# Second mixer of a two-layer decoder: the last gate projection ahead of the second group's scan, and each tile's output chain behind its own chunk

## The chip, the cores and the metric

The kernel runs on one core of a Trainium2 chip. The time is the device time of one execution in microseconds; 3108.14 us is the median of three runs. The core has five engines with instruction streams of their own: TensorE (PE: matmuls and transposes), VectorE (DVE), ScalarE (ACT), GpSimd (POOL) and SyncE (SP), which issues most DMAs. An engine works through its stream in order and waits at an instruction until the semaphores that it names have come.

## The reference

Two layers over 512 tokens of width 1024. In layer 0 the token mixer is a sparse attention, in layer 1 a Mamba-2 scan (SSD); each runs beside a cross-attention of four heads into 256 memory tokens, one output projection takes both, and a PEER block (retrieval of single-neuron experts) follows. The change lies in layer 1:

```python
z, xbc, dt_raw, q_mem = jnp.split(h @ b_w_in[j], B_SPLITS, axis=-1)
...
xbc = jax.nn.silu(causal_depthwise_conv(xbc, conv_w, conv_b))
...
y = ssd_scan(xh, dt, a, bm, cm) + xh.astype(jnp.float32) * d[..., None]
y = y.reshape(b, s, SEQ_WIDTH) * jax.nn.silu(z.astype(jnp.float32))
return rms_norm(y, out_norm).astype(z.dtype)
...
mem_out = memory_attention(q_mem, mem_n, w_mem_kv[i])
x = x + jnp.concatenate([seq_out, mem_out], axis=-1) @ w_o[i]
```

The scan has 12 heads in two groups of 6, and is done in four chunks of 128 tokens; a chunk needs the state that the chunk before it left.

## The kernel before

Tokens are four tiles of 128 (t = 0 to 3). A matmul in full precision is three matmuls of a high and a low half (L70, L71, L72). Layer 1 keeps the normed input transposed (`hT`, a high and a low half), and its steps are emitted in the order of a string, `B_ORDER`, which `run_steps` reads. The framework's scheduler takes the emission order as priority and fixes each engine's stream at build; so a step's instructions end up woven into those of other steps.

The steps: `x(j)` projects a block of 128 columns, convolves it, applies SiLU and transposes it (L679, to `xtm`). `decay(t,g)` makes a chunk's decay factors for group g. `z(1)` and `z(2)` project 256 gate columns each for all four tiles, in two halves of two tiles, evicted by ScalarE (L658, to `zs`). `mem(t)` is the cross-attention of a tile, in two halves of two heads: scores (L331, L332), row maximum (L333), exponential (L337, to `P`), transposes (L341), their eviction (L343, to `PT`), weighted sums into the bank `po` (L347), and the division (L351, to `om`). `chunk(t,g)` is a chunk of the scan: the product of the chunk's C and B (L788), times the decay (L789), the diagonal part into `po` (L792), added to `xtm` (L795); from the second chunk on the part of the state (L798, L800, L802); and but for the last chunk the state's update (L807 to L812). `silu()` applies SiLU to the gates of all four tiles (L704). `out(t)` is a tile's output chain: the gates (L817, GpSimd), the sum of squares (L108, ScalarE), the norm's factor (L96 to L104, with a power on GpSimd, L98), its application (L821), six transposes (L363) and the split into `hT` (L83 by ScalarE, L84 by VectorE). `om_T(t)` transposes the attention's output into `hT`. SiLU and Exp are in different tables of ScalarE, so each change from one to the other is a table load.

PSUM has eight banks, which this layer shares out by kind of use; each kind takes its banks in turn, in the order of emission:

```python
self.use_banks(mm=(4, 5, 0), tr=(6, 7), po=(1,), z=(2, 3))
```

`tr` serves the transposes of the softmax (`mem`), of the output chain (`out`) and of `om_T`; a bank is free again when what was read from it has been read. The sum of squares of `out(t)` writes its squares into one of the three `w_raw` buffers, into which the weight blocks of the output projection are loaded too:

```python
self.sumsq(ss, y, self.scratch()[:, :SW])
```

Behind the steps comes `out_proj`, which accumulates all four tiles over eight blocks of `hT`, the two blocks of `om` (6 and 7) first (`acc`).

Of the kernel before, what the change touches and what calls it, by code (L numbers as in the profile page):

```python
# [35 lines left out]
class Trunk:  # L36
# [522 lines left out]
    def attend(self, work, t, j, qS, kS, bias, v, mask, o):  # L559
# [49 lines left out]
        else:  # L609
# [3 lines left out]
        yield  # L613

    B_ORDER = ("qm(0) decay(0,0) x(6) x(1) x(8) qm(1) decay(1,0) x(0) x(2) decay(2,0) x(7) decay(3,0) x(9) chunk(0,0) "
               "x(3) chunk(1,0) chunk(2,0) z(1) chunk(3,0) decay(0,1) decay(1,1) x(4) x(5) decay(2,1) decay(3,1) mem(0) "
               "chunk(0,1) mem(1) chunk(1,1) mem(2) chunk(2,1) mem(3) z(2) chunk(3,1) om_T(0) om_T(1) silu() out(0) "
               "out(1) om_T(2) om_T(3) out(2) out(3)")

    def layer_b(self):  # L620
        self.use_banks(mm=(4, 5, 0), tr=(6, 7), po=(1,), z=(2, 3))
# [656 lines left out]
```

## Time and profile before

| | |
|---|---|
| median of 3 runs | 3108.14 us (3108.0 to 3112.97) |
| the profiled execution | 3111.33 us |
| its span | 3109.6 us |
| PE busy | 2993.3 us, 96% |
| DVE busy | 2319.9 us, 75% |
| ACT busy | 1288.6 us, 41% |
| POOL busy | 963.0 us, 31% |
| mean granted TensorE clock | 0.988 |

The rows below are of this one execution; times in them are microseconds from the span's start. In a timeline a row begins with start and duration; neighbours on one engine overlap a little, so the step from one start to the next is shorter than the duration. What stands in brackets is the idle time before, and what ended it. In PE's rows a full-precision operand of 4 bytes shows as two passes, so a count there can be twice the program's.

### The profile page before, as it was taken

The numbers are of one execution on the slowest core, as the hardware profiler recorded it, in microseconds if no ns is written. First come the engines' busy times: TensorE is split into PE (matmuls) and PEld (weight loads), VectorE is DVE, ScalarE is ACT, GpSimd is POOL, SyncE is SP. The second block draws the span as 40 slices with busy tenths as digits, with TensorE's granted clock in tenths as the row PEclk, the third lists the DMA queues.
The fourth block names the chain that finished last, engine by engine and source line by source line (L and its number), as shares of the span: only waits on it lengthen the run. The fifth ranks groups of instructions, "written<-read, shape, count | busy, mean of one in ns | idle before, by whom it ended". The sixth has DMA issues, their size and how long they took to land.

```text
span 3109.6 us, 44049 instructions
## 1 busy us (share of the span) xinstructions
PE 2993.3 (96%) x16033; PEld 2585.1 (83%) x16038; DVE 2319.9 (75%) x4553; ACT 1288.6 (41%) x2021; POOL 963.0 (31%) x699
## 2 busy tenths in 40 slices
PE   8899999989999999999999999999999999999998
PEld 7788767778999999999978777667799999999997
DVE  5954899857777777777767659995677777777776
ACT  5574327633333333333345632584333333333332
POOL 3312320003333334444313333001233333444440
PEclk9999999999999999999999999999999999999999
DMA  4311226888888889898721122579789988889983
GB/s 162 104 40 55 75 88 247 312 278 294 310 306 306 303 308 322 305 311 305 235 91 62 50 82 69 184 283 324 258 303 311 321 306 307 305 302 314 319 287 104
DMA packets 235154, 718.61 MB, mean 231 GB/s; under 512 B 21388, under 2 KB 86456, under 8 KB 231864
## 3 DMA queue, kind: packets, MB, share of 16 engines
q1 hardware_dynamic: 155952, 440.01, 39.9%
q0 software_dynamic: 73728, 268.47, 25.6%
q10 hardware_dynamic: 5256, 7.32, 0.8%
q8 instruction: 125, 2.05, 0.3%
q14 instruction: 93, 0.76, 0.1%
HBM read 653.96 MB, written 61.75 MB: 230 GB/s over the span
## 4 chain that ended last, share of the span: by engine, by line
PE 78%; DVE 14%; DMA 3%; issue 3%; ACT 2%; POOL 1%; SPq 0%; POOLq 0%; DVEq 0%; ACTq 0%
PE acc L71 11%; PE acc L70 11%; PE acc L72 11%; PE mm L70 11%; PE mm L71 11%; PE mm L72 11%; PE up L907 4%; PE g L1142 2%; DMA act_r<-ad 1%; DVE tk_s L1034 1%; DVE tki L1037 1%; DMA gt<-gd 1%; DVE tki L1036 1%; PE po L603 1%; DVE score L554 1%
## 5 line engine op out<-in xcount | busy, mean ns | idle before, releaser
L72 PE MATMUL mm<-hT,w_lo 128*128 128x384 f32 (+2 forms) x2104 | 726.2, 345 | 3.0 <-POOL w_lo L84 2.8
L70 PE MATMUL mm<-hT,w_hi 128*128 128x384 f32 (+2 forms) x2104 | 726.9, 346 | 0.5 <-ACT hT L83 0.5
L71 PE MATMUL mm<-hT,w_hi 128*128 128x384 f32 (+2 forms) x2104 | 726.0, 345 | 0.4 <-DVE hT L84 0.4
L84 DVE TENSOR_TENSOR w_lo<-w_raw,w_hi 128x1024 fp32r<-128x1024 f32 (+1 forms) x218 | 267.0, 1225 | 472.9 <-ACT w_hi L83 472.8
L71 PE MATMUL acc<-v_lo,a_hi 128*128 128x512 f32 x1536 | 605.3, 394 | 13.3 <-DVE v_lo L84 13.2
L70 PE MATMUL acc<-v_hi,a_hi 128*128 128x512 f32 x1536 | 603.3, 393 | 12.3 <-issue 12.3
L83 ACT CAST w_hi<-w_raw 128x1024 fp32r<-128x1024 f32 (+2 forms) x311 | 321.9, 1035 | 701.8 <-PE mm L71 578.1
L1156 POOL DMA_INDIRECT row<-in_u,exi x256 | 298.1, 1164 | 1012.9 <-DVE junk L1162 688.5
L72 PE MATMUL acc<-v_hi,a_lo 128*128 128x512 f32 x1536 | 601.4, 392 | 0.0
L1156 POOL DMA_INDIRECT row<-in_v,exi x256 | 397.8, 1554 | 458.1 <-DVE acc L1173 377.7
L70 PEld LDWEIGHTS mm<-hT,w_hi 128*128 128x128 f32 x2104 | 397.2, 189 | 22.7 <-ACT hT L83 1.4
L71 PEld LDWEIGHTS mm<-hT,w_hi 128*128 128x128 f32 x2104 | 396.6, 189 | 22.0 <-DVE hT L84 1.3
L72 PEld LDWEIGHTS mm<-hT,w_lo 128*128 128x128 f32 x2104 | 396.3, 188 | 19.3 <-POOL w_lo L84 6.7
L71 PEld LDWEIGHTS acc<-v_lo,a_hi 128*128 128x128 f32 x1536 | 291.0, 189 | 69.7 <-DVE v_lo L84 16.6
L70 PEld LDWEIGHTS acc<-v_hi,a_hi 128*128 128x128 f32 x1536 | 290.6, 189 | 69.0 <-issue 12.9
L72 PEld LDWEIGHTS acc<-v_hi,a_lo 128*128 128x128 f32 x1536 | 290.7, 189 | 63.0 <-DVE a_lo L84 0.7
L83 ACT CAST a_hi<-ring 128x384 fp32r<-128x384 f32 x214 | 110.0, 514 | 555.7 <-PE acc L71 553.1
L84 DVE TENSOR_TENSOR v_lo<-v_raw,v_hi 128x1024 fp32r<-128x1024 f32 x256 | 312.6, 1221 | 17.1 <-ACT v_hi L83 16.1
L1173 DVE SCALAR_TENSOR_TENSOR acc<-row,gact,acc 128x1024 f32<-128x1024 f32 x252 | 313.8, 1278 | 0.0
L1162 DVE SCALAR_TENSOR_TENSOR junk<-row,h 128x1024 bf16<-128x1024 f32 x256 | 311.6, 1217 | 0.1
L84 POOL TENSOR_TENSOR w_lo<-w_raw,w_hi 128x1024 fp32r<-128x1024 f32 (+3 forms) x93 | 213.9, 2306 | 285.8 <-ACT w_hi L83 266.3
L83 ACT CAST v_hi<-v_raw 128x1024 fp32r<-128x1024 f32 x256 | 268.1, 1047 | 5.0 <-DMA v_raw<-in_v 5.0
(348 smaller groups left out, 3848.9 us busy)
## 6 DMA issues: line engine op xcount, KB each, us to landing
w_raw<-in_uT SPq DMA_DIRECT2D x256, 512.0 KB, 5.2
v_raw<-in_v SPq DMA_DIRECT2D x256, 512.0 KB, 6.5
gd<-st SPq DMA_DIRECT2D x24, 2048.0 KB, 6.8
gt<-gd SPq DMA_DIRECT2D x32, 1536.0 KB, 11.7
w_raw<-in_w_q SPq DMA_DIRECT2D x32, 512.0 KB, 3.2
w_raw<-in_w_o SPq DMA_DIRECT2D x16, 512.0 KB, 3.7
ad<-ring SPq DMA_DIRECT2D x42, 192.0 KB, 3.8
act_r<-ad SPq DMA_DIRECT2D x42, 192.0 KB, 3.4
```

The lines of the kernel that those rows point to most:

```text
L70: mm(out, lhs[0], rhs[0], start=start, stop=False)
L71: mm(out, lhs[0], rhs[1], start=False, stop=False)
L72: self.pe_last = mm(out, lhs[1], rhs[0], start=False, stop=stop)
L83: self.nc.scalar.copy(hi, src)
L84: return (eng or self.nc.vector).tensor_tensor(lo, src, hi.bitcast(F32), OP.subtract)
L554: nc.vector.match_replace(out=sc, in_to_replace=m8, in_values=sc, imm_value=MARK)
L603: nc.tensor.matmul(po[:, i], pts[i][:, b * 128:b * 128 + 128], v[:, b, h * 64:h * 64 + 64], start=b == 0, stop=b == t)
L907: mm = nc.tensor.matmul(p, w[:, k], hw[:, k], start=k == 0, stop=k == KC - 1)
L1142: mm = nc.tensor.matmul(p[:, i], oh[1][:, q + i], oh[k][:, q + i], start=k == 2, stop=k == 3)
L1156: nc.gpsimd.indirect_dma_start(out=g, out_offset=None, in_=I[name], in_offset=bass.IndirectOffsetOnAxis(ap=exi[:, s:s + 1], axis=0))
L1162: nc.vector.scalar_tensor_tensor(j, g, 1.0, h, op0=OP.mult, op1=OP.mult, accum_out=act[:, s:s + 1])
L1173: nc.vector.scalar_tensor_tensor(a, g, act[:, s:s + 1], a, op0=OP.mult, op1=OP.add)
```

## The change

The emission order of layer 1 is changed from the last steps of `decay` on. `z(2)` is emitted ahead of `mem(0)` instead of ahead of the last chunk; `silu()` follows the first chunk of group 1 instead of the last; and `out(0)`, `out(1)` and `out(2)` follow chunks 1, 2 and 3, where all four stood at the end. No step is added or taken out.

```diff
     B_ORDER = ("qm(0) decay(0,0) x(6) x(1) x(8) qm(1) decay(1,0) x(0) x(2) decay(2,0) x(7) decay(3,0) x(9) chunk(0,0) "
-               "x(3) chunk(1,0) chunk(2,0) z(1) chunk(3,0) decay(0,1) decay(1,1) x(4) x(5) decay(2,1) decay(3,1) mem(0) "
-               "chunk(0,1) mem(1) chunk(1,1) mem(2) chunk(2,1) mem(3) z(2) chunk(3,1) om_T(0) om_T(1) silu() out(0) "
-               "out(1) om_T(2) om_T(3) out(2) out(3)")
+               "x(3) chunk(1,0) chunk(2,0) z(1) chunk(3,0) decay(0,1) decay(1,1) x(4) x(5) decay(2,1) decay(3,1) z(2) "
+               "mem(0) chunk(0,1) silu() mem(1) chunk(1,1) out(0) mem(2) chunk(2,1) out(1) mem(3) om_T(0) om_T(1) "
+               "chunk(3,1) out(2) om_T(2) om_T(3) out(3)")
```

On ScalarE, behind the last factors of `decay(3,1)` (L771): before, the first tile's exponentials come at once, and the gates' SiLU is split over the attention.

```order
L771 ACTIVATE cde<-cde 128x6
L337 ACTIVATE P,ms_sum<-mm,ms_max 128x256 x4
L343 COPY PT<-tr 128x512
L658 COPY zs<-z 128x2x256
L343 COPY PT<-tr 128x512
L704 ACT_TABLE_LOAD
L704 ACTIVATE zs<-zs 128x768
L337 ACT_TABLE_LOAD
L337 ACTIVATE P,ms_sum<-mm,ms_max 128x256 x4
```

The same place in the changed program:

```order
L771 ACTIVATE cde<-cde 128x6
L658 COPY zs<-z 128x2x256
L704 ACT_TABLE_LOAD
L704 ACTIVATE zs<-zs 128x768 x2
L658 COPY zs<-z 128x2x256
L704 ACTIVATE zs<-zs 128x768
L337 ACT_TABLE_LOAD
L337 ACTIVATE P,ms_sum<-mm,ms_max 128x256 x3
L343 COPY PT<-tr 128x512
L337 ACTIVATE P,ms_sum<-mm,ms_max 128x256
L704 ACT_TABLE_LOAD
L704 ACTIVATE zs<-zs 128x768
```

Both gate halves, three SiLUs and an Exp load now stand ahead of the first exponential, and the fourth SiLU with its load inside the first tile's softmax.

On PE, the end of the mixer before: the last weighted sums (L347), the state part and the diagonal part of the last chunk (L798, L792), then the transposes of `om` and of all four tiles of `xtm` with the output projection (`acc`) woven in.

```order
L347 MATMUL po<-mvt,PT 128x64 x8
L798 MATMUL mm<-state_14699,ccT 128x384
L363 MATMUL tr<-ident,om 128x128 x4
L792 MATMUL po<-xdt,dec 128x64 x6
L363 MATMUL tr<-ident,xtm 128x128 x12
L363 MATMUL tr<-ident,om 128x128 x4
L363 MATMUL tr<-ident,xtm 128x128 x4
L70 MATMUL acc_16145<-w_hi,hT_87 128x512
L70 MATMUL acc_16146<-w_hi,hT_87 128x512
```

The same place in the changed program, from the diagonal part of chunk 2 on:

```order
L792 MATMUL po<-xdt,dec 128x64 x6
L798 MATMUL mm<-state_14699,ccT 128x384
L363 MATMUL tr<-ident,xtm 128x128 x6
L341 MATMUL tr<-ident,P 128x128 x8
L347 MATMUL po<-mvt,PT 128x64 x4
L363 MATMUL tr<-ident,om 128x128
L347 MATMUL po<-mvt,PT 128x64 x4
L363 MATMUL tr<-ident,om 128x128 x3
L792 MATMUL po<-xdt,dec 128x64 x6
L363 MATMUL tr<-ident,xtm 128x128 x6
L363 MATMUL tr<-ident,om 128x128 x4
L363 MATMUL tr<-ident,xtm 128x128 x6
```

The transposes of tile 1's output (`xtm`, third row) now stand between chunk 2 and the last tile's softmax transposes (L341), and all transposes of `xtm` ahead of the output projection, which follows.

## Rows read from the trace of the kernel before

**Rows 1.** Busy time by stretch of 5 us around the change. Columns: the stretch, its length, then busy us (and instructions) of PE, PE's weight loads, DVE, ACT and POOL, then the granted TensorE clock as a share of full speed, the DMA share and GB/s.

```profile
1755.00:1760.00 5.00, 5.00 (x43) 4.60 (x41) 3.90 (x8) 3.63 (x7) 0.08 (x1) 1.00 0.00 1
1760.00:1765.00 5.00, 3.21 (x26) 2.62 (x24) 3.62 (x9) 3.04 (x7) 3.41 (x2) 1.00 0.25 72
1765.00:1770.00 5.00, 1.38 (x5) 0.94 (x6) 3.69 (x14) 2.82 (x6) 1.20 (x3) 0.77 0.39 141
1770.00:1775.00 5.00, 5.00 (x18) 3.94 (x18) 2.25 (x4) 2.37 (x6) 4.75 (x2) 0.55 0.18 44
```

**Rows 2.** The same view, two stretches ahead of the first PEER block, where PE waits for a norm.

```profile
310.00:315.00 5.00, 0.00 (x0) 0.00 (x0) 5.00 (x4) 1.39 (x3) 3.50 (x2) 0.86 0.39 130
315.00:320.00 5.00, 4.77 (x20) 4.32 (x21) 4.23 (x15) 2.24 (x4) 0.80 (x2) 0.50 0.20 79
```

**Rows 3.** TensorE in order of time: start us, us, engine, line, operation, out<-in, shape, count. The last gate projection (`z<-`) and the transposes of the last convolution block (`tr<-ident,cs`).

```profile
1722.05 0.36 PE L70 MATMUL z<-w_hi,hT 128*128 128x256 f32 x1
1724.66 0.28 PE L72 MATMUL z<-w_hi,hT 128*128 128x256 f32 x1
...
1726.07 0.28 PE L72 MATMUL z<-w_hi,hT 128*128 128x256 f32 x1
...
1728.89 0.60 PE L679 MATMUL tr<-ident,cs 128*128 128x128 f32 x4
```

**Rows 4.** ScalarE in order of time, same columns: the SiLU of the last convolution block (`cs`), the softmax exponentials of the memory attention (`P`), the evictions of their transposes (`PT`) and of a gate half (`zs<-z`), and a table load with the first gate SiLU (`zs<-zs`).

```profile
1727.94 0.63 ACT L675 ACTIVATE cs<-cy 128x512 f32<-128x512 f32 x1
1731.28 0.45 ACT L337 ACTIVATE P<-mm,ms_max 128x256 f32<-128x256 f32 x1
1733.07 0.57 ACT L343 COPY PT<-tr 128x512 f32<-128x512 f32 x1
1733.54 0.59 ACT L658 COPY zs<-z 128x512 f32<-128x512 f32 x1
1735.12 1.28 ACT L704 ACT_TABLE_LOAD   x1
1736.41 0.84 ACT L704 ACTIVATE zs<-zs 128x768 f32<-128x768 f32 x1
```

**Rows 5.** TensorE, the users of the one bank `po`: the weighted sums of the memory attention (L347, 8 rows for half a tile) and the diagonal part of a scan chunk (L792).

```profile
1734.32 1.00 PE L347 MATMUL po<-mvt,PT 128*128 128x64 f32 x8
1735.91 1.00 PE L347 MATMUL po<-mvt,PT 128*128 128x64 f32 x8
1738.34 1.45 PE L792 MATMUL po<-xdt,dec 128*128 128x64 f32 x12
1745.57 1.55 PE L792 MATMUL po<-xdt,dec 128*128 128x64 f32 x12
1754.45 1.45 PE L792 MATMUL po<-xdt,dec 128*128 128x64 f32 x12
1760.48 1.52 PE L792 MATMUL po<-xdt,dec 128*128 128x64 f32 x12 [0.33 <-DVE dec L789]
```

**Rows 6.** VectorE in order of time: the decay product of a chunk (L789), the eviction of an attention tile from `po` (L351), the eviction of a chunk from `po` (L795) and its second sum (L802), one of the small steps of the output norm (L101), its application (L821) and a split into the transposed hidden state (L84).

```profile
1737.35 0.42 DVE L351 TENSOR_TENSOR om<-po,ms_rs 128x256 f32<-128x256 f32 x1
1748.77 0.94 DVE L789 TENSOR_TENSOR dec<-dec,mm 128x768 f32<-128x768 f32 x1
1762.05 0.56 DVE L795 TENSOR_TENSOR xtm<-xtm,po 128x384 f32<-128x384 f32 x1 [0.58 <-PE po L792]
1762.63 0.56 DVE L802 TENSOR_TENSOR xtm<-xtm,yo 128x384 f32<-128x384 f32 x1
1765.88 0.16 DVE L101 TENSOR_TENSOR rs_t<-rs_t,rs_ms 128x1 f32<-128x1 f32 x1
1769.79 1.02 DVE L821 SCALAR_TENSOR_TENSOR xtm<-xtm,rs_r,grow 128x768 f32<-128x768 f32 x1
1771.51 0.69 DVE L84 TENSOR_TENSOR hT<-tr,hT 128x512 fp32r<-128x512 f32 x1 [0.37 <-ACT hT L83]
```

**Rows 7.** GpSimd and ScalarE: the gating product of an output chain (L817), the power in its norm (L98), the sum of squares (L108, two rows) and a cast into the transposed hidden state (L83).

```profile
1763.34 1.81 POOL L817 TENSOR_TENSOR xtm<-xtm,zs 128x768 f32<-128x768 f32 x1 [1.59 <-DVE rs_ms L96]
1765.10 0.55 POOL L98 TENSOR_TENSOR rs_y<-rs_ms,mhalf 128x1 f32<-128x1 f32 x1
...
1765.18 0.84 ACT L108 ACTIVATE w_raw<-xtm 128x768 f32<-128x768 f32 x1 [1.72 <-POOL xtm L817]
1765.93 0.19 ACT L108 ACTIVATION_READ_ACCUMULATOR w_raw<-xtm 128x1 f32 x1
1770.89 0.58 ACT L83 CAST hT<-tr 128x512 fp32r<-128x512 f32 x1 [0.45 <-PE tr L363]
```

**Rows 8.** TensorE at the end of the mixer: the transposes of the last two tiles (`tr<-ident,xtm`) and the first matmuls of the output projection (`acc`).

```profile
1769.74 1.12 PE L363 MATMUL tr<-ident,xtm 128*128 128x128 f32 x4 [0.49 <-DVE hT L84]
1770.51 2.48 PE L70 MATMUL acc<-w_hi,hT 128*128 128x512 f32 x5
1772.79 0.63 PE L363 MATMUL tr<-ident,xtm 128*128 128x128 f32 x2
1773.13 0.80 PE L71 MATMUL acc<-w_lo,hT 128*128 128x512 f32 x1
1774.15 0.79 PE L363 MATMUL tr<-ident,xtm 128*128 128x128 f32 x4
```

**Rows 9.** The page's part 6, DMA issues: the weight blocks of the output projection; KB each and the median us from issue to landing.

```profile
w_raw<-in_w_o SPq DMA_DIRECT2D x16, 512.0 KB, 3.7
```
## The prediction

> **What bounds the kernel now.** The page's busy shares come first: TensorE is busy for 96% of the span, so nearly all of the kernel is a question of how long PE is kept waiting. The change touches one place, the end of the second mixer, so the windows around it come next [rows 1]. PE is full until 1760, at clock 1.00. Then come two thin stretches, 3.21 and 1.38 us of 5, and the clock falls to 0.77 and 0.55: here the output chains of tiles 2 and 3 end the mixer, and the output projection can't start. That tail, some 8 us of waiting and slow clock, is all that can be won.
>
> PE is full before it only because the last gate projection, `z(2)`, is spread through the memory attention and the scan as filler. It has 96 matmuls (4 tiles, 8 slices of D, 3 products); twelve take 1.41 us [rows 3], so it is 11.3 us of filler. The timeline of PE shows what really paces the stretch [rows 5]: the attention's weighted sums and a chunk's diagonal part share one PSUM bank, `po`, and so alternate: sums of tile t, VectorE evicts (0.42), chunk t, VectorE evicts (0.56) [rows 6], sums of t+1. The group's four chunks start at 1738.34, 1745.57, 1754.45 and 1760.48.
>
> **The change, step by step.** No instruction is added; one of ScalarE's table loads goes. I lay the new order out, instruction by instruction on the four engines, with the rows' durations and 0.07 us for each hand-over between engines: the rows have 0.03 (L817 ends 1765.15, L108 starts 1765.18) to 0.15 (L802 ends 1763.19, L817 starts 1763.34) [rows 6, 7]. Back to back an operation costs about 0.09 less than its row says, since neighbours overlap.
>
> 1. *The gates first.* PE is at the first `z(2)` matmul at 1722.05 in both programs. It now meets the transposes of the last convolution block behind 42 of them, at 1727.0, and these wait for the SiLU that ends at 1728.57 [rows 3, 4]: 1.6 us of waiting. With the transposes (0.44, their 0.60 less the overlap) and the other 54 matmuls (6.3), `z(2)` ends at 1735.4.
>
> 2. *ScalarE reaches the softmax late.* The second gate half can be evicted at 1735.56; then the SiLU of tile 2 and an Exp load stand ahead of the first exponential: 0.49 + 0.76 + 1.28 puts it at 1738.1, where before it was at 1731.28 [rows 4]. Behind three exponentials and an eviction stands the SiLU of tile 3 with two more loads (1.28 + 0.76 + 1.28), so tile 0's second half of sums comes at 1743.2 (before 1735.91) and, with 1.00 for the half and 0.42 for L351, chunk 0 at 1744.8 (before 1738.34): 6.5 us late [rows 5].
>
> 3. *Chunks 0 to 2.* The sum of squares of out(0) now stands on ScalarE ahead of tile 1's second eviction. From chunk 0: L792 1.45, L795 0.55, L817 1.82, L108 1.03, eviction 0.57, sums 1.00, 0.6 in VectorE's queue, L351 0.42, and hand-overs: chunk 1 at 1752.7, 7.9 behind (before 7.2). Chunk 2 follows at 1760.1, 7.4 behind (before 8.9), with the casts of out(0) ahead of tile 2's evictions. The scan is then 5.7 us late.
>
> 4. *Chunk 2 to chunk 3, the dear step.* Output chains and softmax take the two `tr` banks in turn, so mem(3)'s transposes now wait until VectorE has split out(1)'s transposes. Chunk 2 ends at 1761.6; VectorE does L795, the products for chunk 3, L802, L789 and one more eviction before L821 of tile 1, which ends at 1766.05. Its transposes end at 1766.9; their cast stands behind tile 2's sum of squares (which waits for L817 of tile 2, 1763.95 to 1765.8) and ends at 1767.6; their split stands behind tile 2's power, four small steps of 0.2 and L821 (1768.5 to 1769.4), and ends at 1770.1. Only now come mem(3)'s transposes (0.60), an eviction (0.57), two halves of sums (0.84 + 1.00), L351 (0.42) and three or four hand-overs: chunk 3 at 1774.0, 13.9 behind chunk 2 (before 6.0) [rows 5 to 7].
>
> 5. *The tail.* Chunk 3 ends at 1775.4; L795 0.47, L802 0.55, L817 1.82, L108 1.03, L98 0.55, four small steps with two splits among them 1.4, L821 1.0, and hand-overs: 1782.8. Tile 3's transposes (0.67) stand ahead of the output projection, so PE must pass them first. Five L70 (0.23 each, twice a matmul of half the columns), and the first L71 is at 1784.7.
>
> *Sum.* Before, the first L71 is at 1773.13, with six transposes still woven in behind it, about 1.2 us [rows 8]; now none is left. At full clock: 1784.7 - 1773.1 - 1.2 = 10.4 us. But PE idles for 7 us ahead of tile 3's transposes, as it did before ahead of the projection, where the clock was 0.55 and five L70 took 2.48 us; that is already inside 1773.13. At half clock the transposes and five L70 take 0.67 + 1.16 = 1.8 more. [...] I take mem(3)'s transposes, one half of the sums and half of L792 at that level: 0.45 + 0.84 + 0.7 = 2.0. Together **+14.2 us**. Bounds: hand-overs of 0.04 or 0.10 move it by 1.0 either way; no slow clock at all leaves 10.4, the slow clock from 1763.5 to the end gives 15.7.
>
> Behind the projection's start the order on every engine is the same. Its first weight blocks go into buffers that the sums of squares use as scratch, so these DMAs move with tiles 1 to 3; tile 1's sum now ends at 1760.1 and a load lands in 3.7 us [rows 9], long before 1783. Without that cover the 3.7 us would be on the path.
>
> The profiled execution took 3111.33 us, span 3109.6; the median of the runs is 3108.14, 0.1% less. On the median the sum gives 3108.1 + 14.2 = **3122.3 us**, 0.46% slower. A measurement of this kernel tells a change from none at about 0.2%, or 6.2 us.
>
> **Rivals.**
>
> *A, the whole scan at half clock.* Without filler, PE has waits in every tile from 1736 on. If the clock fell there, each tile's transposes, sums and L792 (0.44 + 1.68 + 1.33 = 3.4 us on the chain) would double in three more tiles: 14.2 + 10.2 = +24 us, 3132.5. Against it: my layout has 3.6 to 4.4 us of PE work in each 5 from 1740 to 1760, and the stretch with 3.21 still has clock 1.00 [rows 1]. [...] Chance 0.10.
>
> *B, no measurable change: the bank costs little.* If mem(3) waited for out(1) no longer than other things make it wait, chunk 3 would follow chunk 2 after 6.0 us as before, at 1766.1; the tail (8.9 us from chunk 3 to the transposes, 0.67 + 1.16, and 1.8 for the clock) puts the first L71 at 1778.6: 1778.6 - 1773.1 - 1.2 = +4.3 us, 3112.4. For it: of step 4's 13.9 us much is order on VectorE, where a few tenths each way move queues. Against: the order is fixed, and each of the four waits has its instruction. Chance 0.18.
>
> *C, the other side: the bank `po` alone sets the pace.* Sums 1.68, L351 0.42, L792 1.45, L795 0.55 and four hand-overs are 4.4 us per tile; from 1744.8 three of them put chunk 3 at 1758.0, the first L71 at 1768.7, and the time at 1768.7 - 1773.1 - 1.2 = -5.6 us, 3102.5. From chunk 3 at 1757.4 on it is faster by over 0.2%. For it: the chains of tiles 0 to 2 are out of the tail, and a table load is saved. Against: ScalarE needs as much per tile, four exponentials of 0.45, two evictions of 0.48, a sum of squares of 0.93 and casts of about 0.7 [rows 4, 7], and twice it waits for the output chain. Chance 0.08, half of it beyond 0.2%.
>
> The forecast has the other 0.64, in a range of its own from 3117 to 3125 (its bounds).
>
> **How the numbers follow.** Forecast and A are slower: 0.74. B and half of C lie within 0.2%: 0.22. Half of C is faster: 0.04. For eight in ten the range leaves out A and C, takes in B at 3112.4 with a little below it, and above the forecast's bounds 2 us for what the layout missed: 3111 to 3127.
>
> **What would show it.** Step 1: `z(2)` in one block, ending near 1735. Step 2: first exponential near 1738. Steps 3 and 4: L792 of the second group near 1745, 1753, 1760 and 1774 to 1776, and L341 of the last tile waiting for an `hT` split. Tail: the first L71 of `acc` near 1785 to 1790, with no transposes of `xtm` behind it; clock near 0.5 around it. The sum is wrong if chunk 3 comes before 1768, if something else than out(1)'s split is what mem(3) waits for, or if the time behind the mixer moves by itself.

## The result and the profile after

| | before | after |
|---|---|---|
| median of 5 runs | 3108.14 us (3107.0 to 3112.97) | 3130.3 us (3122.09 to 3132.61) |
| the profiled execution | 3111.33 us | 3130.3 us |
| its span | 3109.6 us | 3128.4 us |
| PE, DVE, ACT, POOL busy | 2993.3, 2319.9, 1288.6, 963.0 us | 3004.8, 2323.2, 1287.7, 964.9 us |
| mean granted TensorE clock | 0.988 | 0.983 |

The ratio is 1.0064, 95% interval 1.0053 to 1.0075: slower by 19.9 us of 3108 (16.5 to 23.3). The prediction had the sign, and +14.2.

To place the loss, one ruler serves for all kernels below: the time from the first `z(2)` matmul, which no edit moves against what stands ahead of it, to the transposes of `h` (`tr<-ident,h`), the first of the next block. Before, these are at 1722.05 and 1817.91, so 95.86 us. After, in PE's timeline (columns as in [rows 3]):

```profile
1719.93 0.36 PE L70 MATMUL z<-w_hi,hT 128*128 128x256 f32 x1
...
1743.20 1.55 PE L792 MATMUL po<-xdt,dec 128*128 128x64 f32 x12
...
1751.45 1.45 PE L792 MATMUL po<-xdt,dec 128*128 128x64 f32 x12
...
1765.98 1.54 PE L363 MATMUL tr<-ident,xtm 128*128 128x128 f32 x6 [4.19 <-DVE rs_ms L96]
...
1769.17 1.97 PE L341 MATMUL tr<-ident,P 128*128 128x128 f32 x8 [1.64 <-DVE hT L84]
1771.01 1.97 PE L347 MATMUL po<-mvt,PT 128*128 128x64 f32 x8
...
1775.31 2.82 PE L792 MATMUL po<-xdt,dec 128*128 128x64 f32 x12
...
1787.74 1.52 PE L363 MATMUL tr<-ident,xtm 128*128 128x128 f32 x6 [6.24 <-DVE xtm L821]
1788.90 2.48 PE L70 MATMUL acc<-w_hi,hT 128*128 128x512 f32 x5
1791.18 0.63 PE L71 MATMUL acc<-w_lo,hT 128*128 128x512 f32 x1
...
1835.70 1.07 PE L363 MATMUL tr<-ident,h 128*128 128x128 f32 x8 [0.23 <-issue]
```

1835.70 - 1719.93 is 115.77: the stretch is 19.91 longer, which is the whole loss in time. What lies behind it took 1291.7 us before and 1292.7 after. Chunks 0 and 1 are at 23.27 and 31.52, chunk 2 at 39.06 (its matmuls begin at 1758.99, in two rows); before they were at 16.29, 23.52 and 32.40 [rows 5]. So they are 6.7 to 8.0 late. Chunk 3 follows 16.3 behind chunk 2, where before it took 6.0, and the rows of that stretch have about twice their length: 1.97 for half the sums (1.00 before [rows 5]), 2.82 for L792 (1.52). The windows of 5 us show why (columns as in [rows 1]):

```profile
1755.00:1760.00 5.00, 4.76 (x43) 4.52 (x41) 3.61 (x11) 2.21 (x5) 2.55 (x2) 1.00 0.02 7
1760.00:1765.00 5.00, 1.39 (x7) 0.63 (x5) 5.00 (x11) 2.19 (x9) 2.84 (x2) 0.80 0.29 98
1765.00:1770.00 5.00, 2.38 (x10) 1.98 (x11) 3.58 (x10) 1.35 (x4) 0.55 (x1) 0.50 0.30 105
1770.00:1775.00 5.00, 5.00 (x25) 4.72 (x24) 0.17 (x1) 1.17 (x2) 0.00 (x0) 0.50 0.00 0
1775.00:1780.00 5.00, 4.41 (x21) 3.73 (x19) 2.58 (x6) 1.60 (x4) 0.54 (x1) 0.50 0.02 3
1780.00:1785.00 5.00, 1.11 (x4) 0.67 (x4) 2.66 (x7) 2.41 (x5) 3.02 (x3) 0.50 0.30 103
1785.00:1790.00 5.00, 2.26 (x9) 2.10 (x10) 3.01 (x5) 1.14 (x3) 1.75 (x3) 0.50 0.00 2
1790.00:1795.00 5.00, 5.00 (x16) 3.94 (x15) 0.50 (x2) 0.67 (x1) 2.43 (x1) 0.63 0.80 283
```

From some point in 1760 to 1765 until one in 1790 to 1795 PE is at 0.50, some 30 us; before, it fell and came back within the 10 us from 1765 to 1775 (0.77 and 0.55 [rows 1], then 1.00 in 1775 to 1780):

```profile
1775.00:1780.00 5.00, 5.00 (x24) 4.10 (x23) 1.02 (x2) 1.67 (x3) 1.05 (x3) 1.00 0.80 296
```

And VectorE has steps in the norm's small chain that take 10 to 14 times their length, each beside a GpSimd operation. VectorE, then GpSimd, in order of time:

```profile
1762.98 1.56 DVE L104 TENSOR_TENSOR rs_r<-rs_y,rs_t 128x1 f32<-128x1 f32 x1
...
1783.90 2.25 DVE L101 TENSOR_TENSOR rs_t<-rs_t,rs_ms 128x1 f32<-128x1 f32 x1
...
1786.57 1.02 DVE L821 SCALAR_TENSOR_TENSOR xtm<-xtm,rs_r,grow 128x768 f32<-128x768 f32 x1
```

```profile
1762.72 1.80 POOL L817 TENSOR_TENSOR xtm<-xtm,zs 128x768 f32<-128x768 f32 x1
...
1783.80 2.34 POOL L84 TENSOR_TENSOR w_lo<-w_raw,w_hi 128x1024 fp32r<-128x1024 f32 x1 [0.68 <-ACT w_hi L83]
```

L104 ends with GpSimd's L817 (1764.5), L101 with GpSimd's split of a weight block (1786.1); elsewhere in the mixer they take 0.15 to 0.16 [rows 6]. The whole chain of tile 3 stands behind L101. The trace of the kernel before has one such step too, in the next block, where GpSimd splits two weight blocks; so the effect could be read before the change, and [rows 6] alone did not show it. VectorE, then GpSimd, of the kernel before:

```profile
1819.07 1.96 DVE L104 TENSOR_TENSOR rs_r<-rs_y,rs_t 128x1 f32<-128x1 f32 x1
```

```profile
1818.65 4.66 POOL L84 TENSOR_TENSOR w_lo<-w_raw,w_hi 128x1024 fp32r<-128x1024 f32 x2 [2.83 <-ACT w_hi L83]
```

### The profile page after: what moved, and what is told of

It reads as the page before. It is cut to its first block, busy times and chain, and to the rows that moved or that the text cites. A ratio compares the mean times of both kernels' runs of the same rounds, so it can differ in the third digit from the quotient of the medians.

```text
span 3128.4 us, 44046 instructions
## 1 busy us (share of the span) xinstructions
PE 3004.8 (96%) x16033; PEld 2595.9 (83%) x16038; DVE 2323.2 (74%) x4553; ACT 1287.7 (41%) x2020; POOL 964.9 (31%) x699
## 4 chain that ended last, share of the span: by engine, by line
PE 79%; DVE 13%; issue 2%; ACT 2%; DMA 2%; POOL 1%; SPq 0%; POOLq 0%; ACTq 0%; DVEq 0%
PE acc L71 12%; PE acc L70 12%; PE acc L72 11%; PE mm L70 11%; PE mm L71 11%; PE mm L72 11%; PE up L907 4%; PE g L1142 2%; DVE tk_s L1034 1%; DMA act_r<-ad 1%; PE po L603 1%; DVE tki L1037 1%; DVE tki L1036 1%; PE tr L363 1%; DVE tkv L1033 1%
## 5 line engine op out<-in xcount | busy, mean ns | idle before, releaser
L70 PE MATMUL mm<-hT,w_hi 128*128 128x384 f32 (+2 forms) x2104 | 728.3, 346 | 0.5 <-ACT hT L83 0.5
L71 PE MATMUL mm<-hT,w_hi 128*128 128x384 f32 (+2 forms) x2104 | 727.7, 346 | 0.4 <-DVE hT L84 0.4
L84 DVE TENSOR_TENSOR w_lo<-w_raw,w_hi 128x1024 fp32r<-128x1024 f32 (+1 forms) x218 | 267.0, 1225 | 476.9 <-ACT w_hi L83 476.6
L70 PE MATMUL acc<-v_hi,a_hi 128*128 128x512 f32 x1536 | 602.6, 393 | 13.4 <-issue 13.4
L71 PE MATMUL acc<-v_lo,a_hi 128*128 128x512 f32 x1536 | 604.4, 393 | 10.7 <-DVE v_lo L84 10.6
L83 ACT CAST w_hi<-w_raw 128x1024 fp32r<-128x1024 f32 (+2 forms) x311 | 321.9, 1035 | 705.0 <-PE mm L71 578.0
L70 PEld LDWEIGHTS mm<-hT,w_hi 128*128 128x128 f32 x2104 | 398.3, 189 | 23.1 <-ACT hT L83 1.4
L71 PEld LDWEIGHTS mm<-hT,w_hi 128*128 128x128 f32 x2104 | 397.9, 189 | 22.1 <-DVE hT L84 1.3
L70 PEld LDWEIGHTS acc<-v_hi,a_hi 128*128 128x128 f32 x1536 | 290.2, 189 | 70.1 <-issue 14.0
L71 PEld LDWEIGHTS acc<-v_lo,a_hi 128*128 128x128 f32 x1536 | 290.4, 189 | 66.5 <-DVE v_lo L84 13.6
L83 ACT CAST a_hi<-ring 128x384 fp32r<-128x384 f32 x214 | 110.1, 514 | 556.1 <-PE acc L71 553.4
L84 DVE TENSOR_TENSOR v_lo<-v_raw,v_hi 128x1024 fp32r<-128x1024 f32 x256 | 312.5, 1221 | 15.8 <-ACT v_hi L83 14.6
L84 POOL TENSOR_TENSOR w_lo<-w_raw,w_hi 128x1024 fp32r<-128x1024 f32 (+3 forms) x93 | 213.6, 2302 | 288.9 <-ACT w_hi L83 268.4
L83 ACT CAST v_hi<-v_raw 128x1024 fp32r<-128x1024 f32 x256 | 268.1, 1047 | 5.4 <-DMA v_raw<-in_v 5.4
```

Of the source, the lines that this page charges most:

```text
L70: mm(out, lhs[0], rhs[0], start=start, stop=False)
L71: mm(out, lhs[0], rhs[1], start=False, stop=False)
L83: self.nc.scalar.copy(hi, src)
L84: return (eng or self.nc.vector).tensor_tensor(lo, src, hi.bitcast(F32), OP.subtract)
```

## The experiments

No kernel leaves any of the computation out; where matmuls are added, nobody reads what they make. An edit that adds or removes lines shifts the line numbers (L792 is L789 to L796 below). The table gives starts behind the first `z(2)` matmul, from one profiled execution each, and the ratio to before on the same chip from 5 to 11 executions. The scheduler makes the same program of `e1_z_first` and `e6_z_only`, and their rows agree within 0.06 us up to `h`. `e2` and `e7` agree within 0.04 us only until the same six transposes take 0.88 us in one and 1.43 in the other, and chunk 3 then lies 1.2 us apart (below). So a difference of about 1 us between two rows proves nothing by itself. The ratios' intervals are 6 to 9 us wide, and single executions of one kernel lie up to 11 us apart.

| run | chunk 0 | 1 | 2 | 3 | first L71 | `h` | ratio (95%) |
|---|---|---|---|---|---|---|---|
| before | 16.29 | 23.52 | 32.40 | 38.43 | 51.08 | 95.86 | |
| after | 23.27 | 31.52 | 39.06 | 55.38 | 71.25 | 115.77 | 1.0064 (1.0053 to 1.0075) |
| e1_z_first | 23.31 | 30.24 | 36.80 | 47.04 | 61.51 | 105.51 | 1.0030 (1.0020 to 1.0040) |
| e6_z_only | 23.31 | 30.24 | 36.83 | 47.06 | 61.53 | 105.53 | 1.0034 (1.0023 to 1.0045) |
| e2_out_banks | 23.28 | 31.16 | 37.92 | 50.02 | 65.06 | 109.83 | 1.0037 (1.0024 to 1.0051) |
| e11_gate_on_dve | 23.31 | 30.29 | 40.90 | 49.14 | 62.31 | 106.00 | 1.0038 (1.0025 to 1.0052) |
| e3_lo_on_dve | 23.29 | 31.55 | 39.09 | 55.41 | 69.61 | 113.60 | 1.0051 (1.0037 to 1.0065) |
| e4_keep_clock | 23.31 | 31.57 | 39.10 | 54.89 | 70.44 | 114.06 | 1.0047 (1.0033 to 1.0060) |
| e5_keep_clock2 | 23.30 | 31.55 | 39.08 | 52.92 | 65.91 | 110.94 | 1.0053 (1.0039 to 1.0067) |
| e12_keep_lo | 23.30 | 31.55 | 39.09 | 52.92 | 64.07 | 107.20 | 1.0034 (1.0021 to 1.0048) |
| e7_both | 23.30 | 31.18 | 37.94 | 51.24 | 65.80 | 109.37 | 1.0045 (1.0032 to 1.0059) |
| e9_all_three | 23.31 | 31.18 | 37.95 | 53.36 | 67.91 | 112.17 | 1.0059 (1.0045 to 1.0072) |
| e10_z_first_keep | 23.29 | 30.21 | 39.07 | 52.36 | 65.15 | 109.60 | 1.0050 (1.0037 to 1.0064) |
| e8_silu_held | 20.74 | 27.42 | 34.26 | 40.62 | 59.35 | 110.05 | 1.0032 (1.0020 to 1.0044) |
| b2_z_after_mem2 | 16.31 | 23.54 | 35.97 | 47.83 | 61.24 | 104.49 | 1.0030 (1.0021 to 1.0039) |
| b4_before_keep | 16.30 | 23.53 | 32.43 | 38.46 | 48.83 | 95.25 | 1.0007 (0.9998 to 1.0016) |
| b5_before_gate | 16.26 | 23.49 | 32.14 | 38.33 | 51.66 | 96.46 | 1.0006 (0.9997 to 1.0015) |
| b6_before_gate_lo | 16.27 | 23.50 | 32.16 | 38.35 | 52.11 | 96.65 | 1.0007 (0.9998 to 1.0016) |

**Half of the change alone.** `e1_z_first` has this order; `e6_z_only` has `silu()` behind `om_T(1)` again:

```diff
- z(2) mem(0) chunk(0,1) silu() mem(1) chunk(1,1) out(0) mem(2) chunk(2,1) out(1) mem(3) om_T(0) om_T(1) chunk(3,1) out(2) ...
+ z(2) mem(0) chunk(0,1) silu() mem(1) chunk(1,1) mem(2) chunk(2,1) mem(3) chunk(3,1) om_T(0) om_T(1) out(0) out(1) ...
```

> The gates and both SiLUs stay where the change puts them, but the output chains go back behind the scan, as in the kernel before. First theory (what is dear in the change is the output chains standing between the chunks: they share the two tr banks with the memory attention, and DVE, ACT and PE queues): the chunks lie 6 to 7.5 us apart, chunk 3's diagonal part starts about 29 us behind the first score (change: 42), and the time comes to about 3114 us (3111 to 3118): the late softmax and the lost filler of the gate projection remain. Rival (the lost filler and the late softmax are the cost, wherever the chains stand): no better than the change, 3125 to 3133 us.

> The kernel before with only the gate projection z(2) moved ahead of the memory attention; SiLUs and output chains stay at the end. First theory (in e1_z_first most of the loss, 9.7 us, comes from PE doing the 11.3 us of z(2) ahead of the scan instead of inside its waits): 7 to 9 us slower than before, ratio 1.0022 to 1.003. Rival (e1's loss is the SiLUs and their table loads ahead of the softmax, 3.3 us twice): 3 to 5 us slower, ratio 1.001 to 1.0016.

`e1` lies between its theories: by the ratio it is at the upper edge of the first one's range, 3117.5 on a kernel before of 3108.1, and two of three steps between chunks are as expected, the last is not. The loss splits in two halves, 9.65 us from the early gates (105.51 against 95.86) and 10.26 from the output chains between the chunks (115.77 against 105.51), each with slow clock and held steps in it (for `e1`: 0.50 from 1770 to 1785 in `e6`, the same program, and L104 takes 1.76 in the tail). Putting back the place of `silu()` alone changed no instruction, so `e6` could not tell the SiLUs from the filler; it repeats `e1`. In `e1` the chunks come 6.9 and 6.6 apart, but the last 10.2, for PE waits once more and is at half clock by then (`e6` has 0.81 in 1765 to 1770 and 0.50 in 1770 to 1775):

```profile
1760.68 1.45 PE L789 MATMUL po<-xdt,dec 128*128 128x64 f32 x12
...
1767.88 1.97 PE L347 MATMUL po<-mvt,PT 128*128 128x64 f32 x8 [2.97 <-ACT PT L343]
...
1770.92 2.66 PE L789 MATMUL po<-xdt,dec 128*128 128x64 f32 x12
```

**What ties chunk 3 to the output chain.** `e2_out_banks`, and `e11_gate_on_dve`:

```diff
-            p = self.psum([128, 4, 128], "tr")      # in transpose_o
+            p = self.psum([128, 4, 128], kind)      # "z" for the output chain
```

```diff
-        nc.gpsimd.tensor_tensor(y, y, zs, OP.mult)  # L817
+        nc.vector.tensor_tensor(y, y, zs, OP.mult)
```

> The changed kernel, with the transposes of the output chain in the two PSUM banks of the gate projection, which are free by then, and so apart from the banks of the memory attention. First theory (out(1) and mem(3) are coupled through the two tr banks): chunk 3 starts some 7 to 10 us behind chunk 2 instead of 16.3, and the time falls by 5 to 10 us, to about 3122 us (3119 to 3126). Rival (what holds chunk 3 is the order in the queues of DVE and ACT, not the banks): within 3 us of the change, 3127 to 3133 us.

> The changed kernel with the gating multiplication of the output chain (L817, 128x768) on VectorE instead of GpSimd. First theory (GpSimd's L817 holds VectorE's 128x1 norm step of the tile before, 1.56 us instead of 0.16, and is itself 1.81 where VectorE's 128x768 forms take about 1.0): chunk 3 starts 2 to 3 us earlier behind the first z(2) matmul (52.5 to 53.5 instead of 55.4), the tail's L817 is 0.8 us shorter, hidden layer's transposes at 111 to 113 instead of 115.8. Rival (VectorE's queue is the bound of the stretch; the multiplication only moves its wait into it): within 1 us of the change, 115 to 117.

With banks of its own the chain lets chunk 3 come 12.1 behind chunk 2 instead of 16.3, not the 7 to 10 of the first theory. The rest of the tie is PE's queue: the output transposes stand there ahead of the second half of the sums, and wait for L821.

```profile
1761.01 1.55 PE L792 MATMUL po<-xdt,dec 128*128 128x64 f32 x12
...
1769.17 0.88 PE L363 MATMUL z<-ident,xtm 128*128 128x128 f32 x6 [1.48 <-DVE xtm L821]
1769.88 1.00 PE L347 MATMUL po<-mvt,PT 128*128 128x64 f32 x8
...
1773.11 2.05 PE L792 MATMUL po<-xdt,dec 128*128 128x64 f32 x12 [1.78 <-DVE om L351]
```

By the lengths of these rows the clock held here until 1770 (0.88 for the six transposes and 1.00 for half the sums, where the change has 1.54 and 1.97 at 0.50), so this gain is not the banks' alone: at full clock the step takes 13.8 (`e12`, below), which leaves an estimated 1.7 for them in this execution. `e11` gave more, 9.8 us to `h`, more than either theory: the multiplication takes 0.96 on VectorE instead of 1.81, the norm's steps are not held (L104 0.15), PE's gaps are shorter (0.49 and 1.37 ahead of tile 1's output transposes and of mem(3)'s L341, after the change 4.19 and 1.64) and the clock stays at 1.00 until 1770. VectorE of `e11`:

```profile
1762.37 0.15 DVE L104 TENSOR_TENSOR rs_r<-rs_y,rs_t 128x1 f32<-128x1 f32 x1
...
1772.62 0.96 DVE L817 TENSOR_TENSOR xtm<-xtm,zs 128x768 f32<-128x768 f32 x1
```

It also changed the order (out(0)'s L821 stands on VectorE behind the two sums of chunk 1 now, and chunk 2 comes 1.8 later), so how much is the held steps and how much the order stays open.

**The held step.** `e3_lo_on_dve` takes GpSimd's split out of the tail:

```diff
-                                (128, 2, 512), nc.vector if k == order[-1] else None) for k in ks}
+                                (128, 2, 512), nc.vector if k in (order[0], order[-1]) else None) for k in ks}
```

> The changed kernel, with the low half of the first block of output projection weights made on VectorE instead of GpSimd, so that no GpSimd operation stands beside the small norm steps of the last tile. First theory (VectorE's 128x1 steps wait for GpSimd's operation to end: 2.25 us for one in the change's tail): that step takes about 0.15 us, and the time falls by about 2 us, to 3128 us (3126 to 3129.5). Rival (the long step is not on the path that sets the end): no change, 3130 to 3132 us.

The first theory: chunk 3 is where it was (55.41), the same L101 takes 0.15, and `h` comes 2.17 earlier. VectorE:

```profile
1785.55 0.15 DVE L101 TENSOR_TENSOR rs_t<-rs_t,rs_ms 128x1 f32<-128x1 f32 x1
...
1786.12 1.02 DVE L821 SCALAR_TENSOR_TENSOR xtm<-xtm,rs_r,grow 128x768 f32<-128x768 f32 x1
1787.05 1.22 DVE L84 TENSOR_TENSOR w_lo<-w_raw,w_hi 128x1024 fp32r<-128x1024 f32 x1
```

**The clock.** `e4`, `e5` and `e12` add matmuls to PE's gaps, `e12` with the edit of `e3` as well:

```diff
+            def keep(i):
+                p = self.psum([128, 384], "z")
+                a = (om[:, 2, :128], hT[0][:, 0, 128:256], hT[0][:, 0, 256:384])[i]
+                b = bT[:, 0, :384] if i == 0 else hT[0][:, 0, :384]
+                for _ in range((7, 7, 33)[i]):          # 22 in e12; e4 has two such places, 8 and 23
+                    nc.tensor.matmul(p, a, b, start=True, stop=True)
```

> The changed kernel with 31 matmuls (128x384) added whose result nobody reads, 8 behind the second memory transposes of tile 2 and 23 in the gap ahead of the last tile's output transposes. First theory (the slow clock in the last 25 us of the mixer costs 5 to 7 us): the granted clock stays nearer 1.00 in the windows 1765 to 1795, the sums, the chunk and the first projection matmuls take half their time, and the time falls to about 3124 us (3121 to 3128). Rival (the path runs over VectorE and GpSimd, and the clock costs under 2 us): 3128 to 3133 us.

> The changed kernel with 47 matmuls (128x384) added whose result nobody reads: 7 behind chunk 2, 7 behind the output transposes of tile 1 and 33 behind those of tile 2, so that every gap of PE over 1 us between chunk 2 and the output projection is filled, which the run e4_keep_clock did not reach (it left gaps of 1.66 and 2.62 us, and the clock fell behind each). First theory (the slow clock costs 5 to 6 us of the mixer's tail): granted clock above 0.95 from 1760 to 1795, chunk 3's diagonal part 1.5 us instead of 2.82, and from the first z(2) matmul to the hidden layer's transposes about 110 us instead of 115.8; time about 4 to 6 us under the change's, ratio to before 1.0045 to 1.005. Rival (the time lies in VectorE and GpSimd chains, and the clock is worth under 2 us there): 114 us or more.

> The changed kernel with the unread matmuls of e5_keep_clock2 (22 instead of 33 in the last gap, which is shorter here) and the first low half on VectorE. First theory (the clock, 4.8 us, and the held norm step in the tail, 2.2 us, are two separate terms that the prediction sized too small or left out): 108 to 109.5 us to the hidden layer's transposes instead of 115.8. Rival (they cover each other): 110.5 to 111.

`e4` missed its aim: it left gaps of 1.66 and 2.62 us, and the window 1770 to 1775 is at 0.74, the next at 0.50; 1.7 us came of it. `e5` kept 0.98 to 1.00 up to the last gap (0.68 in the window behind that) and gave 4.83. `e12` kept it throughout:

```profile
1760.00:1765.00 5.00, 4.76 (x42) 4.52 (x41) 3.61 (x10) 2.49 (x7) 2.55 (x2) 1.00 0.09 21
1765.00:1770.00 5.00, 4.76 (x16) 2.56 (x15) 4.96 (x10) 2.18 (x8) 2.84 (x2) 1.00 0.22 84
1770.00:1775.00 5.00, 3.95 (x24) 2.97 (x24) 3.45 (x10) 1.75 (x6) 0.55 (x1) 1.00 0.32 105
1775.00:1780.00 5.00, 4.57 (x38) 4.10 (x38) 2.01 (x5) 1.47 (x4) 0.00 (x0) 1.00 0.01 3
1780.00:1785.00 5.00, 4.58 (x26) 4.21 (x26) 2.23 (x8) 2.85 (x7) 2.38 (x2) 1.00 0.16 29
1785.00:1790.00 5.00, 3.38 (x18) 2.93 (x19) 3.52 (x7) 1.81 (x3) 1.43 (x3) 1.00 0.42 142
```

```profile
1777.54 1.55 PE L796 MATMUL po<-xdt,dec 128*128 128x64 f32 x12 [0.18 <-DVE om L351]
```

`h` comes 8.57 earlier than after the change, a little more than the first theory's 7.0: 2.17 is `e3`'s, and 6.40 (113.60 to 107.20) is the clock's. The two are separate terms, by one execution each; the ratios go the same way (1.0064, 1.0051, 1.0034), but neighbouring intervals overlap. The added matmuls take little or nothing of that back: in front of each long wait they end before what PE waits for does (PE still idles 0.60, 0.38 and 1.82 us behind them).

**Two of three, and three of three.** `e7_both` is `e2` with `e3`; `e9_all_three` adds 39 matmuls to that; `e10_z_first_keep` adds 22 to `e1`.

> The changed kernel with both edits: the output chain's transposes in the gate projection's banks, and the first low half of the projection weights on VectorE. First theory (the bank coupling, 5.9 us of the mixer, and the shared path of VectorE and GpSimd, 2.2 us, are separate terms): they add up, 107.5 to 108.5 us from the first z(2) matmul to the hidden layer's transposes instead of 115.8, ratio to before 1.003. Rival (the second hides behind the first): 109.5 to 110 us, as with the banks alone.

> The changed kernel with the three suspected terms taken away together: 39 unread matmuls in PE's gaps, the output chain's transposes in the gate projection's banks, the first low half of the weights on VectorE. First theory (clock 4.8, banks 5.9, shared path 2.2 us; the bank edit alone already gave back some of the clock, so about 11 together): 104 to 106 us from the first z(2) matmul to the hidden layer's transposes instead of 115.8. Rival (the terms hide one another): 108 to 110 us, as with two of them.

> As e1_z_first, with 22 unread matmuls (128x384) in PE's gaps from chunk 1 to the output chains. First theory (z(2) as filler in the scan is worth its clock: without it PE falls to half speed from chunk 2 on): clock above 0.95 until the output chains, chunk 3 at 43 to 45 us instead of 47, hidden layer's transposes at 101.5 to 103 instead of 105.5. Rival (the scan behind the early gates waits for ScalarE and VectorE, the clock is worth under 1 us): 104.5 or more.

These don't settle what they were made for. `e7` can't tell whether the terms add, since in the tail of `e2` no step is held any more (L101 0.16), so that the edit of `e3` had nothing to give back there. It shows something else: its rows agree with those of `e2` within 0.04 us up to tile 1's output transposes, at 46.1; these take 0.88 in `e2` (above) and 1.43 here, near the 1.54 that they take at 0.50 after the change, so by that length the clock had fallen, and chunk 3 comes 1.2 later. PE, of `e7`:

```profile
1766.00 1.43 PE L363 MATMUL z<-ident,xtm 128*128 128x128 f32 x6 [1.48 <-DVE xtm L821]
```

In `e9` the clock was 1.00 up to 1785 and the stretch still 2.8 longer than in `e7`: seven of its added matmuls (4.7 us) and tile 1's output transposes stand on PE ahead of the last two heads' scores of `mem(3)`, which start at 46.40 instead of 39.30. In `e10` the first half of tile 2's sums starts 1.0 later than in `e1`, behind the added matmuls, and ScalarE has a sum of squares (L108) ahead of the eviction that the second half waits for; chunk 2 is 2.3 late, and by L795 the clock fell all the same (2.66 for chunk 3, where `e6` has 1.45 for chunk 2 at 1.00).

**The SiLUs, the middle, and the kernel before.** `e8_silu_held` has the order of `e6`, and

```diff
+                one = self.small.tile([128, 1], F32, tag="one", name="one")
+                nc.vector.tensor_scalar(one, om[:, 3, :1], 0.0, 1.0, op0=OP.mult, op1=OP.add)
-                    nc.scalar.activation(zs[:, t], zs[:, t], AF.Silu)
+                    nc.scalar.activation(zs[:, t], zs[:, t], AF.Silu, scale=one)
```

`b2_z_after_mem2` emits `z(2)` behind `mem(2)` and `silu()` ahead of `chunk(3,1)`, with the edits of `e2` and `e3`. `b4_before_keep` adds 17 matmuls to the gap in the tail of before, `b5_before_gate` has L817 on VectorE, `b6_before_gate_lo` the edit of `e3` too.

> As e1_z_first (gates first, output chains at the end), but the SiLUs take a scale of 1.0 that is computed from the last memory attention's result, so that ScalarE can't put them and their table loads ahead of the softmax. First theory (of the 9.7 us that the early gates cost, some 3 to 5 are the SiLUs and the two pairs of table loads in front of the softmax): chunk 0's diagonal part starts about 20 us behind the first z(2) matmul instead of 23.3, and the hidden layer's transposes start at 101 to 103 instead of 105.5; time 3 to 4 us under e1. Rival (the loss is PE's: lost filler and the slow clock): chunk 0 comes earlier, but chunk 3 and the hidden layer's transposes don't, 105 to 107.

> A middle way: z(2) stays filler but stands one place earlier than before (behind mem(2) instead of mem(3)), SiLUs ahead of chunk 3, output chains behind chunk 3 with their transposes in the gate projection's banks, first low half on VectorE. Theory (filler in the scan is kept, and the SiLUs no longer hold the last two output chains, so that only tile 3's chain is behind chunk 3): chunks no later than before by more than 1 us, first projection matmul with the low half 2 to 4 us earlier than before, time 3106 to 3110 on a chip where before takes 3110. Rival (any filler given up early is paid in the scan): equal or slower than before.

> The kernel before with 17 unread matmuls (128x384) in PE's 3.3 us gap behind the output transposes of tiles 0 and 1. First theory (PE's half clock in the tail is on the path): transposes and the first projection matmuls at full clock, hidden layer's transposes at 93 to 94.5 us behind the first z(2) matmul instead of 95.9, time 1.5 to 3 us under before, ratio 0.9990 to 0.9995. Rival (the tail waits for VectorE, GpSimd and ScalarE; a faster PE only waits longer): within 1 us of before.

> The kernel before with L817 on VectorE. First theory (its tail is a chain over GpSimd, ScalarE and VectorE, in which tile 2's norm waits behind tile 3's L817 on GpSimd): the last two chains end 1.5 to 3 us earlier, hidden layer's transposes at 93 to 94.5 behind the first z(2) matmul instead of 95.9, time 1 to 3 us under before. Rival (VectorE has the longest queue of the tail already): 95.5 or later.

> As b5_before_gate, and the first low half of the projection weights on VectorE too, so that GpSimd has no operation over 1 us in the tail. First theory (the two 2.6 us operations of GpSimd behind the last chain hold VectorE's evictions): another 0.5 to 1.5 us earlier than b5. Rival (VectorE's added 2 us of work sits on the path): 0.5 to 2 us later than b5.

`e8` fits neither theory: the early SiLUs and table loads do cost the scan 2.6 us at chunk 0 (23.31 against 20.74) and, with the slow clock that follows (0.81 and 0.50 in `e6`, above), 6.4 at chunk 3 (47.04 against 40.62); but held back they set all four gatings in a row at the end, and PE waits 10.59 us for the first of them; `h` is 4.5 later. (Its profiled execution is the slowest of its six, so the ratio is smaller than the row.) GpSimd, then PE, of `e8`:

```profile
1763.89 7.25 POOL L816 TENSOR_TENSOR xtm<-xtm,zs 128x768 f32<-128x768 f32 x4 [9.89 <-ACT zs L703]
```

```profile
1773.53 1.54 PE L363 MATMUL tr<-ident,xtm 128*128 128x128 f32 x6 [10.59 <-DVE xtm L820]
```

`b2`: chunks 0 and 1 as before, but `z(2)` is used up at 28.89 instead of 34.72, and chunk 2 finds half clock, by its length (2.65, before 1.45 at 1.00 [rows 5]). The rival. PE:

```profile
1760.50 2.65 PE L789 MATMUL po<-xdt,dec 128*128 128x64 f32 x12
```

`b4`: with the whole tail of before at full clock, where [rows 1] have 0.77 and 0.55, the first L71 comes 2.25 earlier, `h` only 0.6, and the time is the same: the rival's numbers. Windows:

```profile
1765.00:1770.00 5.00, 3.90 (x25) 3.34 (x24) 4.54 (x9) 1.60 (x3) 3.50 (x2) 1.00 0.48 157
1770.00:1775.00 5.00, 5.00 (x28) 4.05 (x27) 1.90 (x4) 1.73 (x4) 1.89 (x3) 1.00 0.71 221
```

But `b4` is not the clock alone. Its 17 matmuls outlast the gap, so that the transposes of `om` start at 47.71 instead of 46.08, and GpSimd's split of the weights now begins ahead of the last norm, whose first step takes 2.01 instead of 0.15. What full clock by itself would be worth in that tail stays open. GpSimd, then VectorE, of `b4`:

```profile
1764.94 2.42 POOL L84 TENSOR_TENSOR w_lo<-w_raw,w_hi 128x1024 fp32r<-128x1024 f32 x1 [0.90 <-ACT w_hi L83]
```

```profile
1765.37 2.01 DVE L100 TENSOR_TENSOR rs_t<-rs_y 128x1 f32<-128x1 f32 x1
```

`b5` and `b6` gave nothing either; in `b5` the two chains come together in VectorE's queue, and GpSimd's split of the weights holds the last tile's step; `b6`, where none is held, is no earlier. VectorE of `b5`:

```profile
1768.69 2.17 DVE L104 TENSOR_TENSOR rs_r<-rs_y,rs_t 128x1 f32<-128x1 f32 x1
```

No version beat the kernel before.

## Where the prediction was right and where wrong

- **Steps 1 to 3 held.** `z(2)` ends 13.6 behind the start of its first matmul and the chunks start at 23.3, 31.5 and 39.1; worked out were 13.4, 22.7, 30.7 and 38.1. The layout is 1.0 short by chunk 2, half of it already at chunk 0; where it lies was not traced.
- **Step 4 held at full clock:** chunk 3 comes 13.8 behind chunk 2 in `e12`, worked out were 13.9. The number agrees partly by luck: L104, held for 1.57 in `e12` too, is not in the layout, and the way from L821's end to mem(3)'s transposes was 0.8 shorter than worked out (3.3 for 4.1). Its reason is only partly right. mem(3)'s transposes did wait for out(1)'s split, but with that tie taken away `e2` still needs 12.1, so the `tr` banks alone are an estimated 1.7 of the 7.8 that the step lies above before; the waits in PE's queue and GpSimd's L817 in the chain hold it too, and how the rest divides stays open.
- **Step 5's layout held at full clock:** from chunk 3 to the first L71 11.15 in `e12`, worked out were 10.7. Together steps 1 to 5 are 107.20 - 95.86 = 11.3 us, where the sum had 10.4.
- **The failed terms.** The slow clock: the sum has 1.8 + 2.0 = 3.8, with 5.3 as its upper bound; it cost 6.4. No run shows the 2.0, for mem(3)'s transposes, one half of the sums and half of L792, as a term: after the change the transposes, both halves and all of L792 took 1.97, 1.97, 1.81 and 2.82 at 0.50, where `e5` at 1.00 has 1.09, 1.10, 1.00 and 1.55. The working let PE come back in the middle of chunk 3's matmuls, as it had come back before [rows 1]; it stayed at 0.50 through a stretch with 5.00 of 5 us busy, and up to the first L71 (2.48 for the five L70 ahead of it). And a term that wasn't there: the tail's "four small steps" with two splits were priced at 1.4 together, from rows of 0.16 [rows 6], though they run beside GpSimd's operations. One of them took 2.25, worth 2.2 on the path (`e3`). 0.9 + 2.6 + 2.2 is the 5.7 us that the sum lacks; the three add up by construction, being differences between runs.
- **The rivals.** A fell: the chunks 0 to 2 ran at full clock (1.45 to 1.55; 1.00 in the windows from 1740 to 1760). The half clock came behind chunk 2, in five windows at 0.50: in three of them PE had 1.11 to 2.38 us of work, in the two others 4.41 and 5.00. That the time, 3130.3, came near A's 3132.5 is chance. B and C fell with chunk 3's 16.3 us.
- **The range** had slow clock to the end as a bound, sized at 5.3; with the held steps left out, it ended 3.3 us below the median.

## What to carry to other kernels

Filler that stands in a tuned kernel can do more than fill waits. Here the matrix engine also stayed at speed with it: 1.00 up to 1765 before and from 1760 to 1790 in `e12`, 0.50 from 1765 to 1790 after the change. Taking it out ahead of a chain of waits had to be priced at half clock from the first thin stretch through to the output projection, past a window in which PE was full, and not only for the instructions next to the waits. A tiny VectorE step on a chain cost nearly as much here as the GpSimd operation that ran beside it (2.25 for 2.34), so a chain is to be laid out with the neighbour's rows too, and a held step is to be looked for in the whole trace. Moving a chain between two steps that share an in-order queue tied them together even with separate banks (chunk 3 came 12.1 behind chunk 2 in `e2`, before 6.0). And matmuls added to keep the clock had a price where they outlasted the wait (`b4`: the transposes of `om` at 47.71 instead of 46.08) or stood ahead of other work (`e9`: the last scores at 46.40 instead of 39.30).

## What the runs showed of the hardware

- A VectorE operation on 128x1 elements with two operands lasted until GpSimd's operation ended: 1.56 beside L817 (1.80), 2.25 beside the weights' split (2.34), 2.27 in `e8` (2.42), 2.34 in `e5` (2.42); 0.15 with GpSimd out of the way (`e3`). In `e10`, beside one and the same L820, L102 with one operand took 0.15 and L104 with two took 1.54. One step with a single operand of 128x4 was held as well (L96 at 34.60 in the kernel before, 1.67 beside a split of 2.41), so the number of operands is not the whole of it. GpSimd, then VectorE, of `e10`:

```profile
1757.24 1.80 POOL L820 TENSOR_TENSOR xtm<-xtm,zs 128x768 f32<-128x768 f32 x1
```

```profile
1757.33 0.15 DVE L102 TENSOR_SCALAR rs_t<-rs_t 128x1 f32<-128x1 f32 x1
1757.52 1.54 DVE L104 TENSOR_TENSOR rs_r<-rs_y,rs_t 128x1 f32<-128x1 f32 x1
```

- After the change the granted clock stayed at 0.50 in a stretch where PE was busy 5.00 of 5 us, behind two with 1.39 (at 0.80) and 2.38 (at 0.50); in `e12`, where the gaps were filled, it stayed at 1.00 from 1760 to 1790, with 3.38 to 4.76 us of work in each window.
- `e2` and `e7` had the same rows within 0.04 us up to 46.1 and parted there: 0.88 against 1.43 for the same six transposes, and 1.2 us at chunk 3. For six transposes `e5` has 0.88 at 1.00, and the change 1.54 at 0.50.
